# A two-layer trunk on one core: LayerNorm order, modulation rows, late remainders and an epsilon

## The chip, the core and the metric

The kernel runs on one NeuronCore of a Trainium2 chip. The metric is the device time of one execution in microseconds (us), lower is better. TensorE (PE in the profile) does matrix products and transposes, VectorE (DVE) elementwise work and statistics, ScalarE (ACT) activations, casts and copies, GpSimd (POOL) a few small operations, and SyncE (SP) issues the transfers from memory. Each engine works through its own row of instructions in order and waits where an operand is not there yet.

## What is computed

A decoder trunk of two layers over 256 tokens of width 1024, in float32. Layer 0 mixes tokens with block-sparse attention (with 256 tokens it is one causal block), layer 1 with differential attention; each mixer is followed by a dense squared-ReLU MLP of width 4096. The core of the reference, where `c` is a conditioning vector and `sublayer` is the mixer or the MLP:

```python
mod = silu(c) @ ada_w + ada_b          # six vectors per layer: shift, scale, gate, twice
h = x * (1 + scale) + shift
y = sublayer(h)
x = layer_norm(alpha * x + (1 + gate) * y, ln_g, ln_b)   # lax.rsqrt(var + 1e-5)
```

Differential attention also has an RMSNorm per head, with its own `rsqrt(mean + 1e-5)`.

## The kernel before

The tokens are two blocks b of 128 rows, and the width is cut into pieces of 128 columns. Float32 accuracy comes from a split of each operand: `hi` is the value rounded to the matmul's format, `lo` the remainder, and each product is hi·hi + hi·lo + lo·hi (`mm3`, L165). Weights come as 128x2048 tiles `raw` (three buffers). `split_piece` (L127) makes the halves of a 128x1024 piece: ScalarE casts `hi` (L130), VectorE subtracts to get `lo` (L131). There are 196 such pieces. `dense` (L171) runs one product over all pieces k of the width, three matmuls for each k before the next; `dense2` is its form for two output halves (rows at L184).

The work is written out by hand in `PROGRAM`, a list of steps for each layer: V, Q project values and queries with keys, T transposes them (the rotation's VectorE rows are L356 to L359, TensorE's transposes L366), S scores, P the product with the values, F the turning of its result, O the output projection (`ac` holds the result for block 0, `sc` that for block 1), B a boundary, C a closing, U and X the first MLP product and its turning (Y both for two blocks), D and E the second one. Step names carry the block and the group, so Q03 is the fourth query group for block 0. The scheduler takes the steps in this order as priorities, and sets each engine's row by them and by when it thinks that operands are ready.

The modulation vectors are computed on VectorE. A step `ada_rows` (L211) fetches 128 rows of `ada_w` into a 128x1024 tile `aw` and reduces it against the conditioning vector (L216), one column of eight for a vector. `queue_vector` puts these steps into a queue, and `f` steps in PROGRAM (`fill`) take them out one by one, with two `aw` tiles in turn, so two transfers are under way at most. A second kind of 128x1024 tile, "bc" (three buffers), holds the gate and the rows of ln_g and ln_b from a boundary on, and modulation rows of the very first operand before that; between the two it is unused. All weight and modulation transfers share the queue of SP.

A closing (`close`, L588) is, for each block, `layer_norm` and `modulate`. In `layer_norm` VectorE multiplies the product with the gate (L289), adds the residual (L292), takes statistics (L302, L303); then GpSimd adds epsilon and raises to the power −0.5 (`rsqrt_eps`, L277 and L278); VectorE scales the first half of z (L308) and makes a small column `nm` (L310) with which ScalarE scales the second half (L311). In `modulate` TensorE transposes z (L320, two groups of four), ScalarE scales and shifts (L324) and casts to `hi` (L327), VectorE makes `lo` (L328): the operand `hT` of the next product, one half of the width after the other. While the closing of block 0 runs, TensorE has block 1's output product to do. There are three such inner closings (after layer 0's mixer, after its MLP, after layer 1's mixer) at about 135, 321 and 441 us, called closing 0, 1 and 2 here. The last one has another form: `layer_norm` returns early, and L594 and L597 (VectorE) finish the output.

```python
    def rsqrt_eps(dst, src):
        pool_e.tensor_scalar(out=dst, in0=src, scalar1=EPS, scalar2=None, op0=ALU.add)
        pool_e.tensor_tensor(out=dst, in0=dst, in1=nhalf.to_broadcast(list(src.shape)), op=ALU.pow)
```

## Time and profile before

| | us |
|---|---|
| median of 3 runs | 646.49 |
| lowest and highest run | 642.0 and 646.95 |
| the profiled execution, its own time | 643.97 |
| its span, first to last instruction | 641.9 |

The profile is of one execution. Its time is 2.07 us longer than the span, for what lies around the first and the last instruction. The granted TensorE clock was 0.996 on average. In the rows quoted below, a row of the trace has the start and the duration in us, the engine, the line, the operation, the output and inputs by the program's names with the shape, how many instructions were joined to it (x), and in brackets the idle time of the engine before it with what ended that. Rows that join several instructions have their common duration. A row of a window has its bounds, its length, the busy time of the engines (with the number of instructions), the granted clock, the transfer engines' share and GB/s. Matmuls overlap in their pipeline, so a group's durations add up to more than the time between two starts.

### The profile page before, as it was taken

Reading aid. Unit: us, or ns where it says so; the run is one execution under the profiler, and the core shown is the slowest. Engines: PE = TensorE matmul, PEld = TensorE weight load, DVE = VectorE, ACT = ScalarE, POOL = GpSimd, SP = SyncE. Lnnn points to the kernel's source line nnn. Section 1 sums busy time; section 2 is a strip of 40 time slices with the busy share of each in tenths; the row PEclk is TensorE's granted clock in tenths of the full one; section 3 lists DMA queues with packets and bytes.
Section 4 is the critical chain, followed back from the end, with each engine's and each line's share of the span. In section 5 each row is a group of like instructions: output and inputs, shape, how many; then the busy total and the mean of one; then the engine's idle time right before and its main releaser. Section 6 shows DMA issues by size and latency. Waiting matters only on the chain.

```text
span 641.9 us, 8775 instructions
## 1 busy us (share of the span) xinstructions
PE 611.8 (95%) x3140; PEld 502.5 (78%) x3140; DVE 500.2 (78%) x903; ACT 377.0 (59%) x699; POOL 21.8 (3%) x37
## 2 busy tenths in 40 slices
PE   4889999998999999999999999999999999999994
PEld 3667887886888888888877787777788888888883
DVE  4798998879969888887799988987984646565446
ACT  3448666557836555654476666775785556475530
POOL 0000000001000000000000010011100000000002
PEclk9999999999999999999999999999999999999998
DMA  8997998966588998989774966772663764746401
GB/s 289 409 311 282 317 307 296 314 218 229 203 321 315 333 321 308 330 292 336 258 261 153 337 249 243 256 265 84 207 220 116 258 227 144 250 139 208 187 0 66
DMA packets 65941, 158.23 MB, mean 246 GB/s; under 512 B 4041, under 2 KB 21098, under 8 KB 65898
## 3 DMA queue, kind: packets, MB, share of 16 engines
q1 hardware_dynamic: 65898, 157.68, 70.3%
q8 instruction: 24, 0.39, 0.2%
q14 instruction: 19, 0.16, 0.1%
HBM read 156.62 MB, written 1.05 MB: 246 GB/s over the span
## 4 chain that ended last, share of the span: by engine, by line
PE 68%; DVE 15%; DMA 6%; ACT 4%; issue 3%; POOL 3%; SPq 1%; POOLq 0%; DVEq 0%; ACTq 0%
PE ac L184 14%; PE sc L184 10%; PE mm L683 7%; PE tp L683 6%; PE mm L167 5%; PE mm L168 5%; PE mm L169 5%; DVE lo L131 4%; PE mm L688 3%; PE tp L688 3%; DMA aw<-in_ada_w_dram 3%; DVE aw L216 3%; PE sc L414 2%; ACT hi L130 1%; PE tp L397 1%
## 5 line engine op out<-in xcount | busy, mean ns | idle before, releaser
L131 DVE TENSOR_TENSOR lo<-raw,hi 128x1024 fp32r<-128x1024 f32 x196 | 231.8, 1196 | 47.2 <-ACT hi L130 43.5
L130 ACT CAST hi<-raw 128x1024 fp32r<-128x1024 f32 x196 | 201.0, 1035 | 66.2 <-PE sc L184 47.4
L216 DVE CUSTOM_DVE_ANT_0 aw<-aw,sbc,tabT 128x1024 f32<-128x1024 f32 x96 | 121.6, 1279 | 18.9 <-DMA aw<-in_ada_w_dram 18.9
L167 PE MATMUL mm<-hi,hT 128*128 128x512 f32 x224 | 90.7, 405 | 6.6 <-ACT hi L130 3.8
L169 PE MATMUL mm<-hi,hT 128*128 128x512 f32 x224 | 88.9, 397 | 0.0
L168 PE MATMUL mm<-lo,hT 128*128 128x512 f32 x224 | 88.6, 396 | 0.2 <-DVE lo L131 0.2
L683 PE MATMUL mm<-hT,hi 128*128 128x512 f32 x192 | 60.4, 396 | 0.0
L683 PE MATMUL tp<-hT,hi 128*128 128x512 f32 x192 | 60.3, 395 | 0.0
L167 PEld LDWEIGHTS mm<-hi,hT 128*128 128x128 f32 x224 | 42.3, 189 | 16.9 <-ACT hi L130 4.4
L184 PE MATMUL ac<-hi,sTh 128*128 128x512 f32 x160 | 50.8, 395 | 0.0
L184 PE MATMUL ac<-hi,sTl 128*128 128x512 f32 x160 | 50.7, 394 | 0.0
L184 PE MATMUL ac<-lo,sTh 128*128 128x512 f32 x160 | 49.9, 392 | 0.0
L169 PEld LDWEIGHTS mm<-hi,hT 128*128 128x128 f32 x224 | 42.2, 189 | 8.9 <-DVE hT L328 0.4
L168 PEld LDWEIGHTS mm<-lo,hT 128*128 128x128 f32 x224 | 42.3, 189 | 8.6 <-DVE lo L131 0.4
L184 PE MATMUL sc<-hi,sTh 128*128 128x512 f32 x144 | 45.1, 392 | 0.0
L184 PE MATMUL sc<-hi,sTl 128*128 128x512 f32 x144 | 44.6, 391 | 0.0
L184 PE MATMUL sc<-lo,sTh 128*128 128x512 f32 x144 | 44.5, 390 | 0.0
L688 PEld LDWEIGHTS tp<-hT,lo 128*128 128x128 f32 x192 | 34.4, 188 | 7.5
L688 PEld LDWEIGHTS mm<-hT,lo 128*128 128x128 f32 x192 | 34.4, 188 | 7.3
L693 ACT COPY nat<-mm 128x256 f32<-128x256 f32 x24 | 7.8, 376 | 52.4 <-PE mm L683 52.4
L688 PE MATMUL tp<-hT,lo 128*128 128x256 f32 x192 | 36.0, 279 | 0.0
L688 PE MATMUL mm<-hT,lo 128*128 128x256 f32 x192 | 35.9, 279 | 0.0
(153 smaller groups left out, 904.1 us busy)
## 6 DMA issues: line engine op xcount, KB each, us to landing
aw<-in_ada_w_dram SPq DMA_DIRECT2D x96, 512.0 KB, 5.4
raw<-in_mlp_w_up_dram SPq DMA_DIRECT2D x32, 1024.0 KB, 5.6
raw<-in_mlp_w_down_dram SPq DMA_DIRECT2D x32, 1024.0 KB, 5.5
raw<-in_diff_w_in_dram SPq DMA_DIRECT2D x16, 512.0 KB, 5.1
raw<-in_moba_w_in_dram SPq DMA_DIRECT2D x24, 256.0 KB, 5.8
raw<-in_moba_w_in_dram SPq DMA_DIRECT2D x8, 512.0 KB, 4.8
raw<-in_moba_w_out_dram SPq DMA_DIRECT2D x4, 1024.0 KB, 8.6
raw<-in_diff_w_in_dram SPq DMA_DIRECT2D x4, 1024.0 KB, 5.7
```

The lines of the kernel that those rows point to most:

```text
L130: act.copy(out=hi[:, :n], in_=raw_ap)
L131: vec.tensor_tensor(out=lo[:, :n], in0=raw_ap, in1=hi[:, :n], op=ALU.subtract)
L167: pe.matmul(dst, lhsT=xh, rhs=wh, start=start, stop=False)
L168: pe.matmul(dst, lhsT=xh, rhs=wl, start=False, stop=False)
L169: pe.matmul(dst, lhsT=xl, rhs=wh, start=False, stop=stop)
L184: pe.matmul(dsts[h], lhsT=a, rhs=w[:, h * 512:(h + 1) * 512], start=start and k == 0 and i == 0, stop=stop and k == n - 1 and i == 2)
L216: vec.tensor_tensor_reduce(out=aw, in0=aw, in1=sbc, scale=1.0, scalar=adab_cols(l, v)[:, j:j + 1], op0=ALU.mult, op1=ALU.add, accum_out=dst)
L397: pe.transpose(out=tp[:, s_ * P:(s_ + 1) * P], in_=mats[m][:, kb * P:(kb + 1) * P], identity=ident)
L414: pe.matmul(dst[:, kb * P:(kb + 1) * P], lhsT=qk[b, g][rows, i, :], rhs=qk[kb, g][rows, 2 + i, :], start=True, stop=True)
L683: pe.matmul(ps, lhsT=w[k][0][:, c_], rhs=x3[k], start=first, stop=last)
L688: pe.matmul(ps[:, 0:S], lhsT=w[k][1][:, c_], rhs=x3[k][:, 0:S], start=False, stop=False)
L693: act.copy(out=r[:, i * S:(i + 1) * S], in_=ps[:, S:2 * S])
```

## The change

Four things change.

- `close` calls `layer_norm` and `modulate` under the scheduler's high priority (inner closings only).
- The steps of `queue_vector` put three of five of their rows into "bc" tiles and two into "aw" tiles, until the first boundary step; then all go to "aw" tiles.
- `dense` has a form `late`, which runs hi·hi and hi·lo for all k, and then lo·hi for all k (lo is that of the activations, which VectorE makes last). It is used for the first value product of a layer (g2 = 0; layer 0 has another path for it) and the first MLP product (j = 0), for both blocks.
- `rsqrt_eps` adds epsilon on VectorE instead of GpSimd. The power stays on GpSimd.

```diff
-    def dense(dst, lhs, rhs):
+    def dense(dst, lhs, rhs, late=False):
         n = len(lhs)
+        if not late:
+            for k in range(n):
+                mm3(dst, lhs[k], rhs[k], k == 0, k == n - 1)
+            return
         for k in range(n):
-            mm3(dst, lhs[k], rhs[k], k == 0, k == n - 1)
+            for i in range(2):
+                pe.matmul(dst, lhsT=lhs[k][0], rhs=rhs[k][i], start=k == 0 and i == 0, stop=False)
+        for k in range(n):
+            pe.matmul(dst, lhsT=lhs[k][1], rhs=rhs[k][0], start=False, stop=k == n - 1)
...
     filler = deque()
+    spare = {"bc": True, "n": 0}
...
         def step(j):
-            return lambda: ada_rows(l, v, j, cl[:, j:j + 1], "aw", 2)
+            def go():
+                spare["n"] += 1
+                ada_rows(l, v, j, cl[:, j:j + 1], *(("bc", 3) if spare["bc"] and spare["n"] % 5 < 3 else ("aw", 2)))
+            return go
...
     def rsqrt_eps(dst, src):
-        pool_e.tensor_scalar(out=dst, in0=src, scalar1=EPS, scalar2=None, op0=ALU.add)
+        vec.tensor_scalar(out=dst, in0=src, scalar1=EPS, scalar2=None, op0=ALU.add)
         pool_e.tensor_tensor(out=dst, in0=dst, in1=nhalf.to_broadcast(list(src.shape)), op=ALU.pow)
...
-    def unit(w, hT):
+    def unit(w, hT, late=False):
         ps = psum("mm")
-        dense(ps, hT, w)
+        dense(ps, hT, w, late)
         return ps
...
-        z = layer_norm(b, accs, gate)
-        modulate(b, z, A, B, tiles)
+        with tc.high_priority():
+            z = layer_norm(b, accs, gate)
+            modulate(b, z, A, B, tiles)
         filler.appendleft(lambda: residual(b, z, gb, bb))
...
-            ps = unit(w, block_ops(st["x"], b))
+            ps = unit(w, block_ops(st["x"], b), late=g2 == 0)
...
     def step_bound(st, i):
+        spare["bc"] = False
         st["bd"] = boundary(st["l"], i)
...
-        dense(ps, block_ops(st["x"], b), w)
+        dense(ps, block_ops(st["x"], b), w, late=j == 0)
```

The scheduler answers with other rows on the engines. Lines of the changed kernel are 8 to 14 higher: L131 keeps its number, L216 becomes L225, L277 L289, L289 L301, L303 L315, L308 L320, L320 L332, L356 L368, L359 L371 and L184 L192.

The first place is layer 0's attention. On SP, the transfers of the modulation rows (`aw`) stand between those of the weights (`raw`), from about 47 us on, before:

```order
L215 DMA aw<-in_ada_w_dram 128x1024 x2
L145 DMA raw<-in_moba_w_in_dram 128x4x256 x2
L215 DMA aw<-in_ada_w_dram 128x1024
L145 DMA raw<-in_moba_w_in_dram 128x4x256
L215 DMA aw<-in_ada_w_dram 128x1024
L145 DMA raw<-in_moba_w_in_dram 128x4x256
```

and now:

```order
L224 DMA aw<-in_ada_w_dram 128x1024 x8
L145 DMA raw<-in_moba_w_in_dram 128x4x256 x4
L224 DMA aw<-in_ada_w_dram 128x1024 x5
L145 DMA raw<-in_moba_w_in_dram 128x4x256
L224 DMA aw<-in_ada_w_dram 128x1024 x2
L145 DMA raw<-in_moba_w_in_dram 128x4x256 x3
```

Modulation transfers have moved ahead of the weight transfers. On VectorE, the rows ahead of the pieces of Q03's weights (read from raw_1064 and raw_1075), with the numbers of the tiles, were before:

```order
L131 TENSOR_TENSOR lo_1068<-raw_1064,hi_1067 128x1024
L216 ISA aw_775,col02_517<-aw_775,sbc_72,tabT_99 128x1024
L216 ISA col02_517 128x1
L427 RECIPROCAL sums_820<-sums_820 128x4
L356 TENSOR_TENSOR nat_902<-mm_877,cs_71 128x8x16
L357 TENSOR_TENSOR rtmp_903<-mm_877,cs_71 128x8x8
L358 TENSOR_TENSOR rtmp_903<-mm_877,cs_71 128x8x8
L227 TENSOR_SCALAR col02_517<-col02_517 128x8
L216 ISA aw_917,col04_518<-aw_917,sbc_72,tabT_99 128x1024
L216 ISA col04_518 128x1
L359 TENSOR_TENSOR nat_902<-nat_902,rtmp_903 128x8x16
L131 TENSOR_TENSOR lo_1072<-raw_1064,hi_1071 128x1024
```

and are now:

```order
L368 TENSOR_TENSOR nat_975<-mm_950,cs_71 128x8x16
L369 TENSOR_TENSOR rtmp_976<-mm_950,cs_71 128x8x8
L370 TENSOR_TENSOR rtmp_976<-mm_950,cs_71 128x8x8
L225 ISA aw_1003,col04_518<-aw_1003,sbc_72,tabT_99 128x1024
L225 ISA col04_518 128x1
L439 RECIPROCAL sums_932<-sums_932 128x4
L371 TENSOR_TENSOR nat_975<-nat_975,rtmp_976 128x8x16
L131 TENSOR_TENSOR lo_1068<-raw_1064,hi_1067 128x1024
L131 TENSOR_TENSOR lo_1072<-raw_1064,hi_1071 128x1024
L131 TENSOR_TENSOR lo_1079<-raw_1075,hi_1078 128x1024
L491 TENSOR_TENSOR sTl_807<-tp_995,sTh_806 128x2x128
L131 TENSOR_TENSOR lo_1083<-raw_1075,hi_1082 128x1024
```

The first piece of Q03 stood ahead of the rotation of Q12 (nat_902, now nat_975) and stands behind it; nine modulation rows from the queue stood ahead of Q03's last piece, now there are fifteen. On TensorE, Q03's 24 matmuls stood in one run; now one and four of them stand ahead of L366 for Q12 and of attention work, and nineteen behind, with L366 for T03 right after.

The second place is closing 0. VectorE had there:

```order
L289 TENSOR_TENSOR z<-ac,gate 128x512
L216 ISA aw,col_519<-aw,sbc,tabT 128x1024
L216 ISA col_519 128x1
L289 TENSOR_TENSOR z<-ac,gate 128x512
L292 SCALAR_TENSOR_TENSOR z<-x,z 128x512 x2
L302 BN_STATS bns<-z 128x6 x2
L131 TENSOR_TENSOR lo<-raw,hi 128x1024
L216 ISA aw,col_519<-aw,sbc,tabT 128x1024
L216 ISA col_519 128x1
L303 BN_AGGR bna<-bns 128x2
L131 TENSOR_TENSOR lo<-raw,hi 128x1024
```

and has now:

```order
L301 TENSOR_TENSOR z<-ac,gate 128x512 x2
L304 SCALAR_TENSOR_TENSOR z<-x,z 128x512 x2
L314 BN_STATS bns<-z 128x6 x2
L131 TENSOR_TENSOR lo<-raw,hi 128x1024
L315 BN_AGGR bna<-bns 128x2
L131 TENSOR_TENSOR lo<-raw,hi 128x1024
L289 TENSOR_SCALAR rs<-bna 128x1
L131 TENSOR_TENSOR lo<-raw,hi 128x1024
L320 TENSOR_SCALAR z<-z,bna,rs 128x512
```

The modulation rows are gone from the LayerNorm, and the added epsilon row (L289 now) stands behind one whole weight piece and ahead of another. TensorE had there, from the 43rd of the 48 matmuls of block 1's output product on:

```order
L184 MATMUL sc<-hi,sTh 128x512 x2
L320 MATMUL tp<-cs,z 128x128 x4
L184 MATMUL sc<-lo,sTh 128x512 x2
L320 MATMUL tp<-cs,z 128x128 x4
L184 MATMUL sc<-hi,sTl 128x512 x2
L167 MATMUL mm<-hi,hT 128x512
```

and has now, from the 33rd on:

```order
L192 MATMUL sc<-lo,sTh 128x512 x2
L332 MATMUL tp<-cs,z 128x128 x4
L192 MATMUL sc<-hi,sTl 128x512 x2
L192 MATMUL sc<-hi,sTh 128x512
L332 MATMUL tp<-cs,z 128x128 x4
L192 MATMUL sc<-hi,sTh 128x512
L192 MATMUL sc<-lo,sTh 128x512 x2
```

The first transposes stand behind 44 matmuls of that product before and behind 34 now, and between the second group and the next product (L167 before) there are 2 and 11 matmuls. At closing 1 the first transposes stand behind 34 and 39 matmuls, with 3 and 5 more after each group now; at closing 2 behind 34 and 32, with 5 and 11 more after each group now.

## The prediction

> **What bounds the kernel.** I read the busy line of the page and the chain that ended last, then TensorE's busy time in windows around the three inner closings (the LayerNorms that feed another product) and over the attention of layer 0, and last the rows of VectorE and GpSimd in one closing.
>
> ```profile
> PE 611.8 (95%) x3140; PEld 502.5 (78%) x3140; DVE 500.2 (78%) x903; ACT 377.0 (59%) x699; POOL 21.8 (3%) x37
> PE 68%; DVE 15%; DMA 6%; ACT 4%; issue 3%; POOL 3%; SPq 1%; POOLq 0%; DVEq 0%; ACTq 0%
> ...
> 140.00:160.00 20.00, 17.33 (x82) 1.00 0.57 203
> 320.00:350.00 30.00, 28.53 (x135) 1.00 0.62 211
> 440.00:470.00 30.00, 28.75 (x136) 1.00 0.44 141
> ...
> 60.00:97.00 37.00, 36.84 (x215) 29.67 (x213) 35.08 (x89) 24.78 (x62) 0.00 (x0) 1.00 0.85 286
> 97.00:135.00 38.00, 37.21 (x243) 30.93 (x242) 31.56 (x78) 21.53 (x54) 0.00 (x0) 1.00 0.85 291
> ```
>
> TensorE is busy 611.8 of 641.9 us, so an edit gains only what it takes out of the 30 us of idle time, and loses wherever it makes TensorE wait. The closings hold 20.00 − 17.33 = 2.67, 30.00 − 28.53 = 1.47 and 30.00 − 28.75 = 1.25 us of it: 5.39 together, which is all that priority, late remainders and the moved epsilon can win there. In the attention of layer 0 TensorE idles 0.16 us in 37 and 0.79 in 38, beside a VectorE that is busy for 35.08 of the first 37. There the change can win next to nothing, and VectorE has 1.9 us to spare.
>
> The waits of the closings, on TensorE, and the rows of VectorE and GpSimd that make them:
>
> ```profile
> 146.72 0.63 PE L320 MATMUL tp<-cs,z 128*128 128x128 f32 x4 [1.12 <-DVE nm L310]
> 149.85 0.51 PE L167 MATMUL mm<-hi,hT 128*128 128x512 f32 x1 [1.12 <-ACT hT L327]
> ...
> 328.38 0.63 PE L320 MATMUL tp<-cs,z 128*128 128x128 f32 x4 [0.95 <-DVE nm L310]
> ...
> 135.44 0.69 DVE L289 TENSOR_TENSOR z<-ac,gate 128x512 f32<-128x512 f32 x1
> 137.43 1.28 DVE L216 CUSTOM_DVE_ANT_0 aw<-aw,sbc,tabT 128x1024 f32<-128x1024 f32 x1 [1.30 <-DMA aw<-in_ada_w_dram]
> 146.03 0.55 DVE L308 TENSOR_SCALAR z<-z,bna,rs 128x512 f32<-128x512 f32 x1 [0.69 <-POOL rs L278]
> ...
> 320.91 1.29 DVE L289 TENSOR_TENSOR z<-ac,gate 128x512 f32<-128x512 f32 x2
> 324.50 1.21 DVE L131 TENSOR_TENSOR lo<-raw,hi 128x1024 fp32r<-128x1024 f32 x1
> 325.63 0.20 DVE L303 BATCH_NORM_AGGREGATE bna<-bns 128x2 f32<-128x12 f32 x1
> 325.75 1.17 DVE L131 TENSOR_TENSOR lo<-raw,hi 128x1024 fp32r<-128x1024 f32 x1
> 327.69 0.55 DVE L308 TENSOR_SCALAR z<-z,bna,rs 128x512 f32<-128x512 f32 x1 [0.77 <-POOL rs L278]
> 328.15 0.15 DVE L310 SCALAR_TENSOR_TENSOR nm<-bna,rs 128x1 f32<-128x1 f32 x1
> ...
> 326.00 1.00 POOL L277 TENSOR_SCALAR rs<-bna 128x1 f32<-128x1 f32 x1 [169.22 <-DVE bna L303]
> 327.08 0.57 POOL L278 TENSOR_TENSOR rs<-rs,nhalf 128x1 f32<-128x1 f32 x1
> 381.14 0.23 POOL L277 TENSOR_SCALAR ss<-ss 128x2 f32<-128x2 f32 x1 [8.66 <-ACT sq L461]
> 395.09 0.86 POOL L277 TENSOR_SCALAR ss<-ss 128x2 f32<-128x2 f32 x1 [11.94 <-ACT sq L461]
> ```
>
> From the first L289 to L308 closing 1 takes 327.69 − 320.91 = 6.78 us, and closing 0 takes 146.03 − 135.44 = 10.59: a modulation row whose transfer was late and two more of VectorE's long rows stand in between. GpSimd's add lasted 1.00 us beside a running L131 and ended at 327.00, just after that piece's end at 326.92; with nothing beside it the same add took 0.23.
>
> **The change part by part.**
>
> *Priority and epsilon at the closings.* No row is added. The chain from L303 to L308 was 327.69 − 325.63 = 2.06 us. Now the epsilon row on VectorE stands behind a whole L131, and the power follows while the next L131 runs. In the chain: L303 0.12, L131 1.13 and the epsilon row 0.07 (pitches; a row of one column such as L310 is 0.15 long), then L131 1.17, then what the power still takes after it. For that the last closing has the nearest rows:
>
> ```profile
> 635.62 1.41 DVE L594 SCALAR_TENSOR_TENSOR z<-z,bna,bc 128x512 f32<-128x512 f32 x2
> 637.49 1.42 DVE L597 SCALAR_TENSOR_TENSOR z<-z,rs,bc 128x512 f32<-128x512 f32 x2 [0.46 <-POOL rs L278]
> ...
> 635.75 0.71 POOL L277 TENSOR_SCALAR rs<-bna 128x1 f32<-128x1 f32 x1 [7.41 <-DVE bna L303]
> 636.53 0.92 POOL L278 TENSOR_TENSOR rs<-rs,nhalf 128x1 f32<-128x1 f32 x1
> ```
>
> The power beside L594 took 0.92 instead of 0.57 and ended 637.45, 0.42 behind the end of L594 (637.03). So 0.12 + 1.13 + 0.07 + 1.17 + 0.42 + 0.04 (to the start of L308) = 2.95: 0.9 us longer than before. If the power is not held, L308 follows the second L131 at once: 2.49.
>
> [...]
>
> With the priority closing 0 should run like closing 1: 6.78 + 0.9 = 7.7 us from L289 to L308, and the transposes start 0.69 later (328.38 − 327.69), at 8.4. The order shows after how many matmuls of block 1's output product TensorE stands at these transposes; a matmul's pitch is 0.227 us (below, 91.89 to 92.12).
> - Closing 0: behind 34 instead of 44. TensorE is there after 34 × 0.227 = 7.7 and waits 0.7 instead of 1.12. Behind them now 14 matmuls stand ahead of the next product instead of 4, 2.3 us more, and hT's wait of 1.12 is covered. Left over: 0.7, and 0.3 of small gaps, so 1.0 of 2.67. Gain 1.7.
> - Closing 1: behind 39 instead of 34: 8.9 us, no wait for the first transposes (0.95 before). But only 8 matmuls follow, 1.8 us and 0.7 of transposes, against 149.85 − 146.72 = 3.1 that hT took from the transposes: a wait of 0.6 comes back there, and the late order reads the second half of hT 8 matmuls later rather than 12, in front of which ScalarE has a cast of 1 us: 0.7 more. 1.3 of 1.47; gain 0.1.
> - Closing 2: behind 32: 7.3 us, wait 1.1; then 16 matmuls cover hT. Gain 0.2.
>
> Together 2.0 us, with the bounds −1 (the chain's 0.9 uncovered once more) and 5.39.
>
> [...]
>
> *Epsilon in layer 1's attention.* Eight adds on GpSimd, such as those of 0.23 and 0.86 us above, become eight VectorE rows of about 0.1, and VectorE is 78% busy. The heads wait for these sums now and then; I take 0.3 of a possible 8 × 0.23 = 1.8, and −1 for rows queued behind VectorE's pieces.
>
> *Late remainders* move the same matmuls; apart from the closings they cost nothing, as TensorE's work is the same.
>
> *Modulation rows in advance.* Three of five 128x1024 rows go to the three "bc" tiles, so five can be under way instead of two until the first boundary. The rows of VectorE and TensorE there:
>
> ```profile
> L216 DVE CUSTOM_DVE_ANT_0 aw<-aw,sbc,tabT 128x1024 f32<-128x1024 f32 x96 | 121.6, 1279 | 18.9 <-DMA aw<-in_ada_w_dram 18.9
> ...
> 83.65 1.22 DVE L131 TENSOR_TENSOR lo<-raw,hi 128x1024 fp32r<-128x1024 f32 x1
> 86.08 0.26 DVE L356 TENSOR_TENSOR nat<-mm,cs 128x128 f32<-128x128 f32 x1
> 86.59 1.28 DVE L216 CUSTOM_DVE_ANT_0 aw<-aw,sbc,tabT 128x1024 f32<-128x1024 f32 x1
> 87.79 0.28 DVE L359 TENSOR_TENSOR nat<-nat,rtmp 128x128 f32<-128x128 f32 x1
> 88.00 3.49 DVE L131 TENSOR_TENSOR lo<-raw,hi 128x1024 fp32r<-128x1024 f32 x3
> ...
> 91.89 0.39 PE L167 MATMUL mm<-hi,hT 128*128 128x512 f32 x1
> 92.12 0.40 PE L168 MATMUL mm<-lo,hT 128*128 128x512 f32 x1
> 97.34 0.60 PE L366 MATMUL tp<-cs,nat 128*128 128x128 f32 x4
> 98.95 0.66 PE L397 MATMUL tp<-cs,p 128*128 128x128 f32 x4 [0.79 <-ACT qkT L368]
> ...
> 81.19 0.43 SPq L145 DMA_DIRECT2D raw<-in_moba_w_in_dram  x1
> raw<-in_moba_w_in_dram SPq DMA_DIRECT2D x24, 256.0 KB, 5.8
> ```
>
> VectorE waits 18.9 us for such rows in all, which is what the change aims at; but no row of TensorE between 60 and 135 waits for them. Their VectorE time is the same 96 × 1.28, only earlier. The order has 15 of them ahead of the last lo piece of Q03 (the fourth query group's weights) where it had 9: 6 rows at a pitch of 1.20 (86.59 to 87.79) are 7.2 us, against 1.9 to spare. Before, those pieces ended at 91.49 and the product began at 91.89, 0.4 behind. On SP's queue the order puts up to eight of these transfers in a row ahead of weight transfers; a row that waits for VectorE to give its tile back then holds the weights behind it. Q03's last transfer was issued at 81.19 and lands some 5.8 later, at 87.0, a microsecond ahead of VectorE's three pieces at 88.00, so SP can only add to what follows. Walking the new order with the old durations:
> - Q02's first pieces stand behind two rows more: TensorE waits about 1.25, and Q12 ends that much later.
> - L359 for Q12 moves from 87.79 by 7.2 and by Q12's 1.25, to about 96.3. TensorE now has five matmuls of Q03 ahead of that L366 and stands there at 91.89 + 1.25 + 1.14 = 94.3: 2.1 of waiting. Then the first lo piece of Q03 ends at about 98.7 and TensorE waits some 1.55, though some 4.8 us of attention work (its rows' old durations) is pulled ahead of the remaining 19 matmuls.
> - L366 for T03 stands right behind Q03's last matmul, its L359 behind another modulation row: 1.28 and the turning's own rows, about 2.0.
>
> That is 6.9 in all. The attention work that was pulled ahead need not be done later, the 0.79 in front of L397 and other gaps of that stretch vanish, and T03's rows are partly those that Q03 waited for: I take 4.0, and keep 0 and 6.9 as bounds. Gains in the stage's end are none: VectorE has 38.00 − 31.56 = 6.4 us of slack from 97 to 135, so it was not late for the closing but for the one row at 137.43, which the 1.7 above counts.
>
> **Sum.** Against the profiled execution of 643.97 us: + 4.0 − 2.0 − 0.45 − 0.3 = 645.2. The median of the runs shown is 646.49, 2.5 above that execution, and they go from 642.0 to 646.95; about 1%, 6.5 us, is what a measurement of this kernel can tell from no change.
>
> **Rivals.**
> 1. *The early rows hide.* The pieces of Q03 come late, but other work covers it: 643.97 − 2.75 = 641.2. For it: TensorE's order was rearranged with them, by 4.8 us of work. Against: TensorE stood only 0.4 behind the pieces. If the power is not held either and the idle time of all closings goes, 643.97 − 5.39 − 0.75 = 637.8.
> 2. *Slower.* The waits of layer 0's attention come in full, 6.9, and the closings give nothing since the epsilon row behind a whole L131 costs the 0.9 that priority wins: 643.97 + 6.9 = 650.9. It decides if Q03's last lo piece ends beyond about 101 and T03's wait stays at 2.
> 3. *The power is not held by L131.* L308 comes 0.5 earlier at two closings: 644.2. The add that ended with L131 speaks against it.
>
> **Chances.** The forecast, 644.5 to 648: 0.38. Rival 3, 643 to 644.5: 0.12. Rival 1: 0.27, of which two thirds lie below 640.0 (1% under the median) only if gains on layer 0 come that no row shows, such as less waiting for transfers; I give 0.17 to faster by over 1%. Rival 2: 0.23, of which 0.13 is slower by over 1%. Same: 0.70. The range takes in rival 2 and most of rival 1: 638 to 651.
>
> **What would show it.** Right: TensorE's waits for L131's lo and L359 between 80 and 105, absent before; 140 to 160 with about 1 us of idle; GpSimd's power 0.9 to 1.6 us long in the closings; L597 half a microsecond behind L594's pair. Wrong: TensorE as full between 60 and 135 as before, or a VectorE row of the closing that still waits for the modulation transfer.

## The result: 1.1% slower, and the profile after

| | before | after |
|---|---|---|
| median, us | 644.65 (4 runs, 642.0 to 646.95) | 651.77 (4 runs, 650.87 to 652.58) |
| ratio | | 1.0115 (95%: 1.0084 to 1.0146) |
| span of the profiled execution | 641.9 | 650.6 |

The forecast was 645.2 with a range from 638 to 651. The changed kernel lies just above the range, on the side that had the smaller chance. Set side by side by four marks on VectorE, the first L289 (L301 after) of each closing, the two spans differ by 8.7 us:

| stretch | before | after | difference |
|---|---|---|---|
| start to closing 0 | 135.44 | 146.54 | +11.10 |
| closing 0 to closing 1 | 185.47 | 182.46 | −3.01 |
| closing 1 to closing 2 | 119.59 | 120.70 | +1.11 |
| closing 2 to the end | 201.42 | 200.91 | −0.51 |

The page of the changed kernel, its busy line and the group of the modulation rows:

```profile
PE 617.5 (95%) x3140; PEld 505.2 (78%) x3140; DVE 501.7 (77%) x919; ACT 376.9 (58%) x699; POOL 18.1 (3%) x21
...
L225 DVE CUSTOM_DVE_ANT_0 aw<-aw,sbc,tabT 128x1024 f32<-128x1024 f32 x96 | 121.5, 1280 | 8.5 <-DMA aw<-in_ada_w_dram 8.2
```

Windows of TensorE (bounds, length, busy time, granted clock, transfer share, GB/s) in the same kernel, two over layer 0's attention and one from the start of each inner closing:

```profile
80.00:100.00 20.00, 16.57 (x84) 0.92 0.76 277
100.00:120.00 20.00, 17.35 (x100) 0.91 0.82 314
...
146.00:166.00 20.00, 19.54 (x91) 1.00 0.31 106
329.00:359.00 30.00, 29.57 (x142) 1.00 0.67 226
449.00:479.00 30.00, 29.55 (x139) 1.00 0.41 141
```

The change did what it set out to do in two places. VectorE waits 8.5 us for modulation rows instead of 18.9, and TensorE idles 0.46, 0.43 and 0.45 us in the closings, 1.34 instead of 5.39. What it costs stands in the two windows ahead: 3.4 and 2.7 us idle in layer 0's attention where it was 0.8 and 0, and a granted clock of 0.92 and 0.91 there. TensorE's busy time grew by 5.7 us with the same 3140 matmuls: some of them took longer, about half of it by the lower clock, as the next windows show.

The rows of that loss in the changed kernel, first TensorE's timeline:

```profile
94.44 0.40 PE L169 MATMUL mm<-hi,hT 128*128 128x512 f32 x1
97.43 0.80 PE L167 MATMUL mm<-hi,hT 128*128 128x512 f32 x1 [2.60 <-ACT hi L130]
98.53 1.11 PE L378 MATMUL tp<-cs,nat 128*128 128x128 f32 x4 [0.31 <-DVE nat L371]
...
114.62 0.63 PE L378 MATMUL tp<-cs,nat 128*128 128x128 f32 x4 [2.65 <-DVE nat L371]
```

VectorE's timeline, Q03's first three lo pieces and the rotation ahead of T03:

```profile
98.39 3.49 DVE L131 TENSOR_TENSOR lo<-raw,hi 128x1024 fp32r<-128x1024 f32 x3
...
112.51 0.29 DVE L368 TENSOR_TENSOR nat<-mm,cs 128x128 f32<-128x128 f32 x1 [0.49 <-ACT nat L367]
...
112.98 1.28 DVE L225 CUSTOM_DVE_ANT_0 aw<-aw,sbc,tabT 128x1024 f32<-128x1024 f32 x1
...
114.18 0.29 DVE L371 TENSOR_TENSOR nat<-nat,rtmp 128x128 f32<-128x128 f32 x1
```

ScalarE's timeline, the cast of Q03's first piece:

```profile
96.33 1.04 ACT L130 CAST hi<-raw 128x1024 fp32r<-128x1024 f32 x1 [0.56 <-DMA raw<-in_moba_w_in_dram]
```

And SP's issues of the transfers ahead of it (start, time from the first to the last issue):

```profile
78.68 0.39 SPq L145 DMA_DIRECT2D raw<-in_moba_w_in_dram  x1
88.22 1.53 SPq L224 DMA_DIRECT2D aw<-in_ada_w_dram  x2
89.81 1.61 SPq L145 DMA_DIRECT2D raw<-in_moba_w_in_dram  x3
```

Q03's product is ready to go at 94.8 and waits 2.6 us for its first weight piece; the transposes for T03 wait 2.65 us for a rotation that VectorE has cut in two with a modulation row (112.98). The late transfer alone did not make the first wait: ScalarE's cast waited 0.56 us for it, and the next rows of TensorE, the transposes for Q12 at 98.53, needed a rotation that VectorE ended at 98.5, whenever the cast came. Between the two waits, windows of 2 us show the clock:

```profile
94.00:96.00 2.00, 0.83 (x6) 1.00 1.04 364
96.00:98.00 2.00, 0.57 (x1) 0.70 1.09 404
98.00:100.00 2.00, 1.69 (x8) 0.50 1.03 420
100.00:102.00 2.00, 2.00 (x7) 0.50 1.03 422
102.00:104.00 2.00, 2.00 (x15) 0.59 0.83 338
104.00:106.00 2.00, 2.00 (x17) 1.00 0.06 25
```

From 96.8 to 103.6, 6.8 us, TensorE had half its clock: two 128x512 matmuls in a row start 0.43 us apart there (100.30 and 100.73) and 0.23 at 109.76 and 109.99, where the clock is 1.00. Its busy time there times the missing part of the clock, (0.57 + 1.69 + 2.00) × 0.50 + 2.00 × 0.41, gives 2.95 us of work lost, an estimate. Behind the second wait, as long as the first, the clock stayed at 1.00 in this execution. It did not in the second profile of the same kernel (taken beside e10, below), where the clock fell from 95.0 to 101.9 and once more behind the wait for T03:

```profile
110.00:112.00 2.00, 0.11 (x1) 1.00 0.86 291
112.00:114.00 2.00, 1.24 (x7) 0.53 1.02 401
114.00:116.00 2.00, 2.00 (x9) 0.62 1.00 406
```

By the same reckoning that execution lost 3.0 us behind the first wait and 1.4 behind the second. Half is the only other level in these windows (those at 0.70, 0.59, 0.53 and 0.62 hold both), and of the two waits of the first profile, 2.60 and 2.65 us, one had it. The last section has how much idle time was enough.

### The profile page after: what moved, and what is told of

Same layout as the page of the kernel before. It is cut to its first block, busy times and chain, and to the rows that moved or that the text cites. A ratio compares the mean times of both kernels' runs of the same rounds, so it can differ in the third digit from the quotient of the medians.

```text
span 650.6 us, 8758 instructions
## 1 busy us (share of the span) xinstructions
PE 617.5 (95%) x3140; PEld 505.2 (78%) x3140; DVE 501.7 (77%) x919; ACT 376.9 (58%) x699; POOL 18.1 (3%) x21
## 4 chain that ended last, share of the span: by engine, by line
PE 57%; DVE 10%; DMA 4%; POOL 1%; issue 1%; ACT 1%; SPq 0%; DVEq 0%; POOLq 0%; ACTq 0%
PE ac L192 12%; PE sc L192 11%; PE mm L697 7%; PE tp L697 6%; PE mm L702 3%; PE tp L702 3%; DVE lo L131 3%; DMA aw<-in_ada_w_dram 3%; PE mm L180 2%; PE mm L169 2%; PE mm L168 2%; DVE aw L225 2%; PE mm L167 2%; DMA raw<-in_diff_w_in_dram 1%; PE sc L426 1%
## 5 line engine op out<-in xcount | busy, mean ns | idle before, releaser
L131 DVE TENSOR_TENSOR lo<-raw,hi 128x1024 fp32r<-128x1024 f32 x196 | 232.0, 1198 | 53.1 <-ACT hi L130 49.6
L225 DVE CUSTOM_DVE_ANT_0 aw<-aw,sbc,tabT 128x1024 f32<-128x1024 f32 x96 | 121.5, 1280 | 8.5 <-DMA aw<-in_ada_w_dram 8.2
L167 PE MATMUL mm<-hi,hT 128*128 128x512 f32 x176 | 71.7, 409 | 7.0 <-ACT hi L130 5.1
L168 PE MATMUL mm<-lo,hT 128*128 128x512 f32 x176 | 70.6, 403 | 0.2 <-DVE lo L131 0.2
L169 PE MATMUL mm<-hi,hT 128*128 128x512 f32 x176 | 70.1, 399 | 0.0
L192 PE MATMUL ac<-hi,sTh 128*128 128x512 f32 x160 | 50.7, 396 | 0.0
L192 PE MATMUL ac<-hi,sTl 128*128 128x512 f32 x160 | 50.2, 393 | 0.0
L192 PE MATMUL ac<-lo,sTh 128*128 128x512 f32 x160 | 49.8, 392 | 0.0
L167 PEld LDWEIGHTS mm<-hi,hT 128*128 128x128 f32 x176 | 33.4, 191 | 15.2 <-ACT hi L130 6.3
L192 PE MATMUL sc<-hi,sTh 128*128 128x512 f32 x144 | 45.2, 392 | 0.0
L192 PE MATMUL sc<-lo,sTh 128*128 128x512 f32 x144 | 44.8, 391 | 0.0
L192 PE MATMUL sc<-hi,sTl 128*128 128x512 f32 x144 | 44.5, 390 | 0.0
L168 PEld LDWEIGHTS mm<-lo,hT 128*128 128x128 f32 x176 | 33.5, 191 | 7.1 <-DVE lo L131 0.4
L169 PEld LDWEIGHTS mm<-hi,hT 128*128 128x128 f32 x176 | 33.4, 190 | 6.6
L396 ACT ACTIVATE p<-sc,mx 128x128 f32<-128x128 f32 (+1 forms) x64 | 26.7, 424 | 18.7 <-DVE mx L393 17.6
```

Of the source, the lines that this page charges most:

```text
L131: vec.tensor_tensor(out=lo[:, :n], in0=raw_ap, in1=hi[:, :n], op=ALU.subtract)
L167: pe.matmul(dst, lhsT=xh, rhs=wh, start=start, stop=False)
L168: pe.matmul(dst, lhsT=xh, rhs=wl, start=False, stop=False)
L169: pe.matmul(dst, lhsT=xl, rhs=wh, start=False, stop=stop)
L192: pe.matmul(dsts[h], lhsT=a, rhs=w[:, h * 512:(h + 1) * 512], start=start and k == 0 and i == 0, stop=stop and k == n - 1 and i == 2)
L225: vec.tensor_tensor_reduce(out=aw, in0=aw, in1=sbc, scale=1.0, scalar=adab_cols(l, v)[:, j:j + 1], op0=ALU.mult, op1=ALU.add, accum_out=dst)
```

## The experiments

All ratios are to the kernel before, run beside each of them on the same chip, with their 95% intervals. "Closing 0 at" is the start of that closing in the profiled execution.

| run | ratio | closing 0 at, us |
|---|---|---|
| e1: changed kernel, no "bc" tiles | 0.9977 (0.9955 to 0.9999) | 134.66 |
| e2: "bc" tiles alone | 1.0167 (1.0141 to 1.0193) | 146.92 |
| e3: priority alone | 1.0118 (1.0092 to 1.0143) | 135.67 |
| e4: epsilon alone | 1.0036 (1.0011 to 1.0061) | 134.60 |
| e5: priority and late order | 1.0002 (0.9968 to 1.0036) | 134.54 |
| e6: late order alone | 1.0017 (0.9977 to 1.0057) | 134.66 |
| e7: priority and epsilon | 1.0116 (1.0062 to 1.0171) | 134.56 |
| e8: changed, first wait filled | 1.0139 (1.0068 to 1.0210) | 149.04 |
| e10: changed, both waits filled | 1.0076 (1.0061 to 1.0091) | 143.02 |
| changed kernel again, beside e10 | 1.0141 (1.0117 to 1.0166) | 145.70 |
| e9: changed, modulation on another queue | 1.0236 (1.0208 to 1.0265) | 150.66 |
| e11: the same, without "bc" tiles | 1.0271 (1.0222 to 1.0319) | 155.13 |
| e12: changed, weights first on SP | 1.0184 (1.0147 to 1.0221) | 150.90 |
| e13: changed, one row of five | 1.0168 (1.0119 to 1.0216) | 146.77 |
| e14: e12 and pieces, rotation first | 1.0114 (1.0079 to 1.0150) | 145.46 |
| e15: e14 without "bc" tiles | 1.0181 (1.0149 to 1.0212) | 137.58 |
| e1 again | 0.9972 (0.9954 to 0.9990) | 134.47 |
| e16: e1, heads' epsilon on GpSimd | 0.9949 (0.9927 to 0.9971) | 134.75 |

### Which part loses: e1 to e4

e1 switches off the tiles, e2 adds them alone to the kernel before:

```diff
-    spare = {"bc": True, "n": 0}
+    spare = {"bc": False, "n": 0}
```

> The changed kernel with all modulation rows in "aw" tiles again. Theory A (the loss comes from the rows in advance alone, by late weights, and TensorE's clock falls after the long wait): closing 0 begins at about 135.5 us instead of 146.5, the granted clock between 80 and 120 is 1.00, and the time is 1 to 4 us under the kernel before (ratio 0.994 to 0.998). Theory B (priority, late order and epsilon also cost, in layer 1's attention, where the changed kernel lost 1.1 us between the second and the third closing): 0 to 2 us over the kernel before.

> The kernel before with the modulation rows in "bc" tiles and nothing else. Theory A: the whole loss without the gains, closing 0 at 146 to 147 us, a time 9 to 12 us over the kernel before (ratio 1.014 to 1.019), above the changed kernel's. Theory B: less than the changed kernel's loss, 5 to 7 us.

Theory A held for both. Without the tiles closing 0 starts at 134.66, the clock is 1.00 and the kernel is 0.2% faster than before; with the tiles alone it starts at 146.92 and 1.7% is lost. The rows in advance make the whole loss, and the rest of the change wins 0.2%.

e3 and e4 make one edit each in the kernel before, the priority and the epsilon row:

```diff
+        with tc.high_priority():
+            z = layer_norm(b, accs, gate)
+            modulate(b, z, A, B, tiles)
...
-        pool_e.tensor_scalar(out=dst, in0=src, scalar1=EPS, scalar2=None, op0=ALU.add)
+        vec.tensor_scalar(out=dst, in0=src, scalar1=EPS, scalar2=None, op0=ALU.add)
```

> The kernel before with the priority of the inner closings alone. If priority alone makes the gain of closing 0 (3.0 us between the first and the second closing in the changed kernel): 2 to 3 us under the kernel before. If it needs the epsilon row on VectorE or the late order: 0 to 1 us under it.

> The kernel before with the epsilon row on VectorE alone. The last closing's L597 should start about 0.45 us earlier behind L594 than before. Theory A: 0 to 1 us under the kernel before in all. Theory B (the rows stand behind VectorE's weight pieces, in front of powers that the heads of layer 1 wait for): 0.5 to 1.5 us over it, between 350 and 440 us.

Both expectations were missed: each alone is slower. TensorE's timeline at closing 0 in e3:

```profile
148.00 0.50 PE L167 MATMUL mm<-hi,hT 128*128 128x512 f32 x1 [0.28 <-ACT hT L327]
...
152.07 0.52 PE L169 MATMUL mm<-hi,hT 128*128 128x512 f32 x1 [3.09 <-DVE hT L328]
...
154.07 1.11 PE L320 MATMUL tp<-cs,z 128*128 128x128 f32 x4 [1.05 <-DVE z L308]
```

and in e4:

```profile
146.47 0.63 PE L320 MATMUL tp<-cs,z 128*128 128x128 f32 x4 [0.81 <-DVE nm L310]
...
149.60 0.79 PE L167 MATMUL mm<-hi,hT 128*128 128x512 f32 x1 [1.59 <-ACT hT L327]
```

Its window there:

```profile
140.00:160.00 20.00, 17.35 (x71) 0.83 0.59 198
```

With priority alone VectorE takes block 1's LayerNorm ahead of block 0's remainder (L328). The next product starts on the rounded half and stops at its third matmul, which reads that remainder, for 3.09 us, and then runs at half clock (0.83 on the mean of 140 to 160). With the epsilon row alone the idle time at closing 0 is that of the kernel before (2.65 and 2.67 us), but its longest wait is 1.59 instead of 1.12 and the clock falls: 0.83 of 20 us, 3.4 us. The kernel before, with waits of 1.12 and 1.12, kept 1.00 there. What e4's expectation said of the last closing held: L597 comes half a microsecond earlier.

### What the late order is for: e5 to e7

All three start from e1. e5 has the epsilon back on GpSimd, e6 also leaves out the priority, and e7 keeps both and leaves out the late order:

```diff
-            ps = unit(w, block_ops(st["x"], b), late=g2 == 0)
+            ps = unit(w, block_ops(st["x"], b))
...
-        dense(ps, block_ops(st["x"], b), w, late=j == 0)
+        dense(ps, block_ops(st["x"], b), w)
```

> Priority and late order, epsilon on GpSimd, modulation rows in "aw" tiles. Priority alone was 1.2% slower, with a wait of 3.3 us for the operand's remainder at closing 0 and half the clock for 7 us behind it. Theory A (the late order takes that wait away, as TensorE reads the remainders 16 matmuls later): no such wait, clock 1.00 between 140 and 160, 0 to 2 us under the kernel before. Theory B (the epsilon row on VectorE is what mends it, by another order of the rows): the wait is still there, 5 to 8 us over the kernel before.

> The late order alone. Theory A: the waits at the closings are for the transposes and for the rounded half, which the late order doesn't touch, so the closings' idle time stays within 0.5 us of 5.39 and the time within 1 us of the kernel before. Theory B (it mends by itself what TensorE waits for): 1.5 to 3 us under it.

> Priority and the epsilon row on VectorE, without the late order, modulation rows in "aw" tiles. Theory A (the late order is needed): a wait of 2 to 4 us between the first matmuls of the next product at closing 0, half the clock behind it, 4 to 8 us over the kernel before. Theory B: none of it, 1 to 3 us under the kernel before.

Theory A held for the times of e6 and e7; e5 was to be 0 to 2 us under the kernel before and is 0.5 over it by the medians, with an interval that takes in both. With the late order beside the priority (e5) the 3 us wait is gone, without it (e7) it is 2.75 us and the clock is 0.83 again, and alone (e6) it changes nothing that can be measured in the time. e6's closings idle 6.1 us, 0.7 over the 5.39 before and so outside theory A's 0.5: at closing 1 its transposes wait 2.47 us for the LayerNorm. The priority is worth having only with the late order: the three together (e1) gain 0.2%, none of e3 to e7 gains anything.

### What the clock costs: e8 and e10

e8 adds 12 matmuls ahead of Q03's product, e10 also 12 ahead of T03's transposes; both write to a tile that is overwritten.

```diff
+            if (l, g, b) == (0, 3, 0):
+                for i in range(12):
+                    pe.matmul(ps, lhsT=st["x"][0][:, 0, 0:P], rhs=st["x"][0][:, 1, :], start=True, stop=True)
```

> The changed kernel with 12 matmuls more, 2.7 us of work, whose result is overwritten, at the one place where TensorE waited 2.6 us for the first weight piece of Q03. No other row of any engine moves. Theory A (the wait cost twice, since the clock was halved behind it): the wait is filled, the clock between 80 and 120 is 1.00, and the time is 2 to 3.4 us under the changed kernel. Theory B (what the slow clock cost is taken by the later wait for T03 in any case): the clock is 1.00 and the time is within 1 us of the changed kernel, with a longer wait in front of T03's transposes. Theory C (the clock falls for another reason): the clock stays at 0.91 to 0.92 there.

> The changed kernel with 12 matmuls more, whose result is overwritten, at each of its two long waits (Q03's first piece, T03's transposes). With the first alone the clock fell behind the second wait instead (half from 112 to 122 us). Theory A (each of these two waits can lower the clock, whichever the clock's window catches): the granted clock is 1.00 from 80 to 140, and the time is 2 to 4 us under the changed kernel's. Theory B (the clock falls for another reason): a stretch of half clock again, and the changed kernel's time or more.

> The changed kernel itself, beside the three others on the same chip: 1.0115 times the kernel before again, half clock for 6 to 10 us between 94 and 125 us.

e8 missed all three theories. In the profiled execution the added rows fill the first wait to the end, and the clock stays up there; but it falls behind the second wait instead, and for longer. One of e8's four executions kept its clock (0.997 on average) and took 647.91 us, the others, at 0.986 to 0.989, took 653.6 to 655.6. The added row, the first wait and the second in e8:

```profile
94.72 2.89 PE L646 MATMUL mm<-hT 128*128 128x512 f32 x12
97.45 0.39 PE L167 MATMUL mm<-hi,hT 128*128 128x512 f32 x1
...
112.69 0.75 PE L378 MATMUL tp<-cs,nat 128*128 128x128 f32 x4 [2.65 <-ACT hi L130]
```

Windows of 2 us behind that second wait:

```profile
112.00:114.00 2.00, 1.31 (x7) 0.77 0.87 293
114.00:116.00 2.00, 2.00 (x7) 0.50 0.97 328
...
122.00:124.00 2.00, 2.00 (x8) 0.67 0.00 0
```

With both filled (e10) theory A held, with a little more than it gave: the clock is 1.00 from 80 to 140, closing 0 starts 2.7 us earlier than in the changed kernel beside it, and the median is 4.2 us lower (647.60 to 651.81). So holding the clock up is worth 2.7 us net in the stage. That is less than the 4.4 us which the windows of the profile beside it give, in part since the added rows and the waits left beside them (0.60 and 0.26 us) take 6.3 us where the waits took 5.4. The other 1.4 us lie between closing 1 and closing 2 (119.3 against 120.7 us); the part on layer 1's attention below has the wait that is missing there. The changed kernel beside e10 took the time that it had taken at first (651.81 and 651.77); its ratio is higher since the kernel before was faster there. The waits themselves are still there in e10, filled with useless work: closing 0 starts 7.6 us later than before.

### What makes the waits: e9 and e11 to e15

The trace offers two causes for Q03's wait: SP, where the weights were issued at 89.81 behind modulation transfers whose tiles VectorE had not yet given back, and VectorE, where seven modulation rows stand ahead of the pieces between 86.9 and 98.4.

e9 and e11 issue the modulation transfers from GpSimd's queue.

```diff
-        sp.dma_start(out=aw, in_=ada_wt[l, r0:r0 + P, :])
+        (sp if early or not spare["bc"] else pool_e).dma_start(out=aw, in_=ada_wt[l, r0:r0 + P, :])
```

> The changed kernel, but until the first boundary the modulation transfers are issued from GpSimd's queue, so that no weight transfer stands behind one of them on SP; the scheduler then puts fewer modulation rows ahead of Q03's pieces on VectorE. Theory A (on SP, a modulation transfer that waited for its tile held Q03's weights, which ScalarE's cast then waited for): Q03's cast no longer waits for its transfer, no wait over 1 us of TensorE between 80 and 120, closing 0 at 134 to 137 us, and a time 0 to 3 us under the kernel before. Theory B (VectorE's time is what lacks, wherever the transfers are issued): closing 0 at 140 us or later, 3 us or more over the kernel before.

> The changed kernel without "bc" tiles for modulation rows, their transfers on GpSimd's queue until the first boundary. Theory A: two tiles are enough once nothing is held behind them, so the time is within 1 us of the same kernel on SP's queue (ratio to the kernel before 0.996 to 0.999). Theory B (more rows in advance would gain once they hold no weights): the kernel with "bc" tiles on GpSimd's queue is 1 us or more faster than this one.

Theory B has the times of both, but they answer nothing on the question: the queued transfers then start at 38 us instead of 48, and TensorE, in e9, is busy for 16.15 us between 60 and 80 instead of 19.84. They are the two slowest kernels of the study.

e12 gives the transfers of layer 0's query weights priority on SP, and e14 also the pieces' cast and remainder and the rotation rows; e15 is e14 without "bc" tiles. e13 is the changed kernel with one row of five in advance.

```diff
+                with (tc.high_priority() if first else nullcontext()):
+                    sp.dma_start(out=r3[:, :, o:o + n],
...
+                with (tc.high_priority() if first else nullcontext()):
+                    hi, lo = split_piece(raw[:, q * 1024:(q + 1) * 1024])
...
+        with (tc.high_priority() if st["l"] == 0 else nullcontext()):
+            act.copy(out=n3[:, :, ROT:], in_=p3[:, :, ROT:])
...
-                ada_rows(l, v, j, cl[:, j:j + 1], *(("bc", 3) if spare["bc"] and spare["n"] % 5 < 3 else ("aw", 2)))
+                ada_rows(l, v, j, cl[:, j:j + 1], *(("bc", 3) if spare["bc"] and spare["n"] % 5 < 1 else ("aw", 2)))
```

The first hunk is e12's, the next two come with e14, and the last is e13's.

> The changed kernel with layer 0's query weights ahead of the modulation transfers on SP (their transfers alone have priority). VectorE's row still has the modulation rows ahead of Q03's lo pieces. Theory S (SP's queue made Q03 late: its weights were issued 8.6 us later than before, behind modulation transfers that waited for their tiles): ScalarE casts Q03's weights by 91 us instead of 96.3, TensorE's waits between 80 and 120 shrink to under 2 us, the clock stays at 1.00 there, and the time is within 2 us of the kernel before. Theory V (VectorE's row made it late: six modulation rows more, 7.2 us, ahead of the pieces): the cast is early, but the lo pieces still end at 98 us or later, TensorE still waits 2 to 3 us at Q03 or T03, and the time is 4 to 9 us over the kernel before.

> The changed kernel with one of five modulation rows in a "bc" tile instead of three, so that three can be under way instead of five. Theory S and V alike: fewer rows go ahead, so the waits between 80 and 120 are smaller (0 to 3 us), too short for the clock to fall, and the time is 0 to 3 us over the kernel with none (e1, 0.2% under the kernel before). Theory D (any row in advance disturbs as much): 6 us or more over the kernel before.

> As the kernel with the weights first on SP, and layer 0's weight pieces (cast and remainder) and rotation rows have priority too, so that Q02's and Q03's pieces stand ahead of the bulk of the modulation rows on VectorE; three of five modulation rows are still in "bc" tiles. Theory V (the modulation rows ahead of Q03's pieces on VectorE made the waits): Q03's pieces end before TensorE needs them, there is no wait over 1 us at Q03 or T03, the clock is 1.00 from 80 to 120, and the time is between 3 us under and 1 us over the kernel before. Theory W (the rows in advance only move their delay to VectorE's next consumers, scores and softmax): a wait of 2 us or more elsewhere between 60 and 140, and 3 us or more over the kernel before.

> The same priorities with all modulation rows in "aw" tiles, two under way. Theory V: within 1 us of the kernel with "bc" tiles and the same priorities. Theory W: 2 us or more faster than it.

The wait in e12, from TensorE's timeline:

```profile
106.04 0.80 PE L170 MATMUL mm<-lo,hT 128*128 128x512 f32 x1 [3.40 <-DVE lo L132]
```

Those in e13:

```profile
94.78 0.63 PE L378 MATMUL tp<-cs,nat 128*128 128x128 f32 x4 [1.91 <-DVE nat L371]
...
109.94 0.63 PE L378 MATMUL tp<-cs,nat 128*128 128x128 f32 x4 [2.40 <-DVE nat L371]
```

Those in e14:

```profile
106.06 0.63 PE L382 MATMUL tp<-cs,nat 128*128 128x128 f32 x4 [1.33 <-DVE nat L375]
...
121.53 1.09 PE L382 MATMUL tp<-cs,nat 128*128 128x128 f32 x4 [2.65 <-DVE nat L375]
```

and VectorE's timeline ahead of the second of them:

```profile
116.37 0.08 DVE L228 DVE_READ_ACCUMULATOR2_ANT col<- 128x1 f32 x1
119.43 0.29 DVE L372 TENSOR_TENSOR nat<-mm,cs 128x128 f32<-128x128 f32 x1 [2.97 <-ACT nat L371]
...
119.90 1.27 DVE L228 CUSTOM_DVE_ANT_0 aw<-aw,sbc,tabT 128x1024 f32<-128x1024 f32 x1
...
121.10 0.28 DVE L375 TENSOR_TENSOR nat<-nat,rtmp 128x128 f32<-128x128 f32 x1
```

e12 settles the first wait for VectorE (theory V): the weights come early (the last casts start at 77.9 us), and TensorE waits all the same, 3.4 us, for a lo piece that stands behind modulation rows. Its loss, 12.5 us, is above theory V's 4 to 9: from 105.0 to 125.5 us TensorE has half its clock. e14 takes the pieces out from behind the modulation rows, and Q03's wait goes; but the transposes of T03 and T13 then wait 1.33 and 2.65 us, the second with a modulation row inside the rotation again (theory W). e13 followed neither S nor V: its waits of 1.91 and 2.40 us are within their 0 to 3, but the clock fell (0.77 on the mean of 100 to 120), and one row of five in advance costs as much as three (theory D), again by two waits for the rotation. In the changed kernel, e13 and e14 one picture returns: transposes that stand close behind the product that they turn, and 1.3 to 2.65 us of waiting for copy and rotation. In the changed kernel, e13 and e14 a modulation row inside the rotation is 1.2 us of the longest wait. VectorE is not out of time there (in e14 it idles 2.97 us just ahead); the rows stand in a bad order. e15 missed both theories by its time, since TensorE waited 11.13 us in closing 0. Up to closing 0, though, it is 7.9 us ahead of e14 (137.58 against 145.46 us): with the same priorities, the rows in advance still cost the stage about that much.

### What became of layer 1's attention: e16

```diff
-            rsqrt_eps(sums, sums)
+            rsqrt_eps(sums, sums, pool_e)
```

> The changed kernel without modulation rows in "bc" tiles once more, beside the two others: 0.2% under the kernel before (ratio 0.995 to 1.000).

> The changed kernel with modulation rows in "aw" tiles only and with the epsilon of layer 1's heads back on GpSimd; the LayerNorms keep theirs on VectorE. Theory E (layer 1's attention lost about 2 us in the changed kernel since two of the heads' powers there are held by VectorE's long rows, 1.5 and 1.7 us instead of 0.7): TensorE's stretch from closing 1 to closing 2 is 1 to 2 us shorter than e1's 120.4 and the time 0.4 to 0.7% under the kernel before. Theory F (the priority reorders that stage, whatever the epsilon does): the stretch stays within 0.5 us of 120.4 and the time at e1's 0.2 to 0.3% under the kernel before.

In the changed kernel two of the heads' powers lasted 1.53 and 1.65 us instead of 0.7, beside VectorE's long rows (L131 at 429.38, 1.22 us, and L225 at 441.16, 1.27), and I took these for the 2 us. e16 puts the heads' epsilon back, its powers are all 0.71 long, and the stretch from closing 1 to closing 2 is 120.68 us, e1's being 120.44: theory F by the length of the stretch, though one wait for the heads did become shorter (below). e16's time is the lowest of all, 0.5% under the kernel before, but its span is e1's within 0.3 us, so that it is better than e1 isn't shown. Both beat the kernel before and the changed one.

## Why the prediction was wrong, step by step

**Layer 0's attention, the term that failed.** The walk through the new order found 6.9 us of waits, and its places were right: 2.60 and 0.31 us at Q03 (3.65 forecast), 2.65 at T03 (2.0 forecast), and 0.53 at Q02 (1.25 forecast), 6.1 together. By the profile it was ScalarE's cast that ended the longest wait at Q03, with the rotation that the walk named 1.1 us behind it, and a pT of ScalarE's, not a weight piece, that ended the one at Q02. Q03's first lo piece ended at 99.6, within 0.2 us of the walk's 98.7 but for the 1.1 us that this execution lost before 20 us, where nothing had changed: its first rows of x came 1.46 us later, and the second profile of the same kernel lost nothing there. Three steps failed.
- The clock was not priced at all. By the windows it took 2.95 us of the stage in the first profile and 4.4 in the second; holding it up (e10) brought 2.7.
- "I take 4.0", on the ground that the work pulled ahead need not be done later, that the 0.79 in front of L397 vanishes and that the waits share their causes. The 0.79 did vanish; nothing else came back, and 6.1 − 0.8 = 5.3 us of waits are left. The attention work that was pulled ahead had stood between Q03's product, which ended at 97.3 in the kernel before, and T03's transposes (at 104.11, the row below). Without it these stand directly behind the product and wait for its copy and rotation.
- The new order itself was booked at nothing. Another 1.7 us of the stage are neither idle time nor clock, but longer steps of TensorE between the same matmuls in another order. No run takes these apart.

```profile
104.11 0.60 PE L366 MATMUL tp<-cs,nat 128*128 128x128 f32 x4
```

Together, 5.3 + 2.95 + 1.7 and the 1.1 at the start are the 11.1 us where 4.0 were forecast; the second profile has 10.3, with 0.6 won at the start. "VectorE's time is the same, only earlier" was right, and "SP can only add" too, but SP turned out not to be needed for the wait (e12).

**The closings** had the right mechanism and too small a gain: 4.05 of idle time instead of 2.0. The chain was right to 0.02 us, and from L289 to the transposes it is 8.36 us against 8.4 forecast. These are the LayerNorm's rows at closing 0 on VectorE:

```profile
151.27 0.20 DVE L315 BATCH_NORM_AGGREGATE bna<-bns 128x2 f32<-128x12 f32 x1
...
154.20 0.55 DVE L320 TENSOR_SCALAR z<-z,bna,rs 128x512 f32<-128x512 f32 x1 [0.45 <-POOL rs L290]
```

on GpSimd:

```profile
152.78 1.39 POOL L290 TENSOR_TENSOR rs<-rs,nhalf 128x1 f32<-128x1 f32 x1 [151.94 <-DVE rs L289]
```

and on TensorE:

```profile
154.90 0.63 PE L332 MATMUL tp<-cs,z 128*128 128x128 f32 x4 [0.46 <-DVE nm L322]
```

L315 to L320 is 2.93 us (2.95 forecast). The power lasted 1.39 us beside an L131 of 1.22 (at 152.54), where it had taken 0.57 at closing 1 before (327.08), with VectorE idle: rival 3 fell. What was too dark is what follows: of the 1.3 forecast at closing 1, a wait for hT, nothing is there, and 0.43 is left in the whole stage; closing 2 has 0.45 where 1.1 was forecast. e7, without the late order, waits 3.24 us for the remainder of hT at closing 1, so the late order is at least part of what covers it. These are figures of single executions: the second profile of e1 waits 1.99 us for the first transposes at closing 1, the first one 0.22.

**Tail.** The forecast's sum has 0.45 for L597. What that takes for the end of the power, the end of VectorE's pair beside it, no run shows: in the changed kernel the power ended at 646.02 (645.10 and 0.92 long) and L606's pair at 646.28, in e4 they ended at 640.17 and 640.43. What the runs showed is that L609 follows that pair without a gap:

```profile
644.87 1.41 DVE L606 SCALAR_TENSOR_TENSOR z<-z,bna,bc 128x512 f32<-128x512 f32 x2
646.19 1.41 DVE L609 SCALAR_TENSOR_TENSOR z<-z,rs,bc 128x512 f32<-128x512 f32 x2
```

The 0.46 us in front of it are gone, and e4, with the epsilon row alone, has the same gain of half a microsecond from the last closing on. The size was right.

**Epsilon in layer 1's attention** was forecast at −0.3. The stretch behind closing 1 became 1.1 us longer although closing 1 itself won 1.0 us, so the attention lost about 2. It did so in e1, e4 and e16 too (120.4, 121.0, 120.7 us against 119.6), but not in e10, where closing 1 is as fast (119.3). Outside the closing TensorE idles 3.22 us in this stretch, 1.50 before. Two waits of the changed kernel make most of that:

```profile
370.82 0.63 PE L378 MATMUL tp<-cs,nat 128*128 128x128 f32 x4 [0.99 <-DVE nat L371]
443.58 0.63 PE L484 MATMUL tp<-cs,on 128*128 128x128 f32 x4 [1.28 <-DVE sums L448]
```

The first, for a rotation, is in e1 (0.87) and e16 (0.90) and neither in the kernel before nor in e10. The second was 0.69 in the kernel before:

```profile
431.55 0.44 PE L472 MATMUL tp<-cs,on 128*128 128x128 f32 x2 [0.69 <-ACT gate L117]
```

It is 1.26 in e1 and 0.70 in e16, so the heads' epsilon on VectorE costs about 0.6 at this wait, where 0.3 of gain was forecast in all. What sets off the first is not shown.

**Late order** at no cost of its own: right (e6). That the priority would need it (e3, e7) was not seen; the forecast took the parts one by one, and the priority alone would have lost 1.2%.

**The sum** by the four stretches is + 11.1 − 3.0 + 1.1 − 0.5 = 8.7, the difference of the spans. Put together by parts it is + 11.1 − 4.05 − 0.5 + 2.1, the same; that they agree is partly luck, as the stretch behind closing 0 won 0.8 us more than its idle time and the last one 0.8 less. The rival that came nearest is the second, 6.9 of waits in full, but it had neither the clock nor the closings' gain: its 650.9 is close to the measured time because two errors offset each other.

## What to carry to other kernels

A wait that a walk through the new order finds on a full engine should be booked in full until the work that covers it has been named; work that is moved ahead to fill one hole leaves another where it stood. Waits of TensorE such as those at which the clock fell here, 1.7 us or more within 3.4 us, should also be priced for the clock: by the estimates above it cost 3.0 to 4.4 us more in one stage, depending on the execution. Judge the parts of a change in the company that they need: priority lost 1.2% alone and gained with the late order, and the prefetch, whose own transfers did come earlier, was the whole loss.

## What the runs showed of the hardware

The granted clock fell to half after some waits and not after others of the same length: after 2.60 us at 97 but not after 2.65 at 114 in the first profile of the changed kernel, at both places in the second, after 0.81 and 1.59 us close together in e4, and not after 1.12 and 1.12 in the kernel before. The kept traces have a pattern in this. In each, all changes of the clock from the first recorded one (at 15 to 18 us) to the fall at the kernel's end lie whole multiples of 3.41 us apart: in the kernel before they are at 15.82 and 637.04 us (182 times 3.41), in the changed kernel at 18.29, 96.80, 103.63 and 646.35 (23, 2 and 159 times). The stretches of half clock last 3.41 (e1 again), 6.83 (the changed kernel) or 10.24 us (e8), and 20.48 in e12. Laid on this grid, the 3.41 us ahead of each of the 19 falls hold 1.68 to 3.41 us in which TensorE idled, 1.97 at 96.80 in the changed kernel and 2.65 at 113.1 in e8; such a stretch is what e10's theory A calls the clock's window. Four stretches with 1.73 to 1.96 us of idle time were followed by no fall, and no stretch with less than 1.68 was. Where the grid lies against the kernel differs from execution to execution (falls at 96.8 and 95.0 in the two profiles of the changed kernel). T03's wait of 2.65 us was cut by it into 1.90 and 0.75 in the first profile and had 1.99 in one stretch in the second; e7's 3.24 us at closing 1 were cut into 1.51 and 1.73, and no fall followed. With both waits filled with matmuls whose result is thrown away, the clock stayed at 1.00 from 80 to 140 (e10).
